# The second MLP matrix of a decoder block: the seven products of a unit in another order

## The chip, the cores and the metric

The kernel runs on one core of one Trainium2 chip. The metric is the device time of one launch in microseconds (us), lower is better; it is taken over several runs, and the median is given with the lowest and the highest. A profile shows one further execution of the same program with every instruction's start and length on the core's engines: TensorE (PE; its weight loads are listed apart, as PEld), VectorE (DVE), ScalarE (ACT), GpSimd (POOL) and SyncE (SP). SP and POOL serve here mainly as queues from which transfers are issued.

## What is computed

One layer of a decoder block for 512 tokens of width 2048, in float32: a mixing part (gated convolution beside attention), then a dense MLP with a squared ReLU, then a last normalisation. The change lies in the MLP:

```python
h = rmsnorm(x, g_mlp[l])
u = jnp.square(jax.nn.relu(jnp.einsum('bsd,df->bsf', h, w_ff1[l])))
x = x + jnp.einsum('bsf,fd->bsd', u, w_ff2[l])
return rmsnorm(x, g_final)
```

`w_ff1` is 2048 x 8192 and `w_ff2` 8192 x 2048. The second product, `u` times `w_ff2`, is "the second MLP matrix".

## The kernel before

**Seven products in place of eight.** Matrix products are cut into 2 x 2 blocks, and a block product is made with seven multiplications of sums of blocks (the Strassen-Winograd scheme). The kernel names the multiplications after the operand on the side of `u`: A11, A12, A22 are blocks of `u` themselves, S1 to S4 are sums of blocks. On the side of the weights, A11 is multiplied with the block X00, A12 with X10, S4 with X11, S1 with X01 - X00, S3 with X11 - X01, S2 with X11 - (X01 - X00), called t2, and A22 with X10 - t2.

**Float32 from two parts.** Each weight operand is split before it is multiplied (`split`, line 99, called by `run`, line 970): ScalarE copies it, rounded, into `th`, and VectorE writes the remainder into `tl`. There are two buffers of each. `mm_rows` (line 145) then issues 24 matmuls of 128x512 a product, for each of two halves of the tokens eight with `th` (lines 156 and 157) and four with `tl` (line 159).

**Sums on the side of `u`.** While the first MLP matrix runs, `put_u` (line 829) squares the results, makes the sums S1 to S4 and stores all seven operands side by side in one DRAM tile per segment (`s_d`, seven places of 256 columns). `load_sums` (line 896) brings them back through POOL's queue in four transfers of neighbouring places, into the four tiles that the table `US` (line 894) names: two operands, two, two, and one. Each tile is free again when its last product of the segment before is done.

**Units.** The second matrix runs over eight segments of 1024 rows of `w_ff2` and, in each, over two groups of 1024 columns: 16 units (`unit`, line 954). A unit

- loads its four blocks of `w_ff2` through SP's queue (line 967), in the order of the loop in line 962, into four rotating buffers; a buffer goes back to the list `free` after the last use of its block, and the next unit's loads take the buffers in the order in which they were given back;
- runs the seven products (lines 989 to 1018) into three PSUM tiles: `a` takes A11, S2, S1 and S4 one on top of the other, `d` takes S3 and A22, `b` takes A12 and is kept through all segments;
- between products overwrites blocks with their differences (`sub`, line 103: X00 becomes X01 - X00, X01 becomes X11 - X01, and t2 is a tile of its own), and adds the PSUM tiles into the output rows held in SBUF (`into`, line 978; line 107 is the addition). In the first segment the first write of each output quarter is a copy on ScalarE.

In the last segment the evictions do more: `residual` (line 940) loads the residual stream in a piece (`old`, on POOL's queue) and adds it to the rows, and `finish` (line 929) scales and adds the last product, has ScalarE sum the squares, and multiplies with the final gain. After the last unit the rows are normalised and written out, rows 2 and 3 of four first.

**What sets the order.** The code gives the instructions of all engines in one sequence. When the program is built, each engine's queue is put in an order by the code's sequence and by when operands are expected to be ready, so a queue may hold a later instruction of the code ahead of an earlier one. On the chip each engine works its queue in that order, with waits on the others.

Of the kernel before, what the change touches and what calls it, by code (L numbers as in the profile page):

```python
# [11 lines left out]
AF = mybir.ActivationFunctionType  # L12
# [33 lines left out]
def tile_hybrid_block(ctx: ExitStack, tc, x, g_mix, w_in, b_f, b_gate, conv_w, w_conv_out,  # L46
                      w_attn_out, w_mix_out, g_mlp, w_ff1, w_ff2, g_final, out):
    nc = tc.nc
    x, out = x[0], out[0]
# [49 lines left out]
    def split(src, hi, lo):  # L99
        nc.scalar.activation(out=hi, in_=src, func=AF.Copy)  # L100
        nc.vector.tensor_tensor(out=lo, in0=src, in1=hi.bitcast(F32), op=ALU.subtract)  # L101

    def sub(out, a, b):
        nc.vector.tensor_tensor(out=out, in0=a, in1=b, op=ALU.subtract)  # L104

    def add(out, a, b):
        nc.vector.tensor_tensor(out=out, in0=a, in1=b, op=ALU.add)  # L107

    def parts(shape, at=0):

        q, w = shape[1:]
        return tuple(main.tile([P, WBUF], F32R, tag=tag, name=tag, bufs=2)[:, at:at + q * w]
                     .rearrange("p (q c) -> p q c", q=q) for tag in ("th", "tl"))
# [31 lines left out]
    def mm_rows(ps, Sx, hi, lo, first):  # L145

        nq, w = hi.shape[1], hi.shape[2]
        for b in range(2):
            o = ps[b][:, :w] if len(ps) == 2 else ps[0][:, b * w:(b + 1) * w]
            begin = first and (b == 0 or len(ps) == 2)  # L150
            ts = slice(b * P, (b + 1) * P)
            for part in range(2):
                for q in range(nq):
                    Sh, Sl = (e[:, ts] for e in Sx(q))
                    if part == 0:
                        nc.tensor.matmul(o, Sh, hi[:, q, :], start=begin and q == 0, stop=False, skip_group_check=True)  # L156
                        nc.tensor.matmul(o, Sl, hi[:, q, :], start=False, stop=False, skip_group_check=True)  # L157
                    else:
                        nc.tensor.matmul(o, Sh, lo[:, q, :], start=False, stop=q == nq - 1, skip_group_check=True)  # L159
# [6 lines left out]
    free, later = [0, 1, 2, 3], []  # L166
# [159 lines left out]
    def rstd_of(part):  # L326
        v = stat.tile([P, 1], F32, tag="v", name="v")
        nc.vector.tensor_reduce(out=v, in_=part, axis=AX.X, op=ALU.add)
        r = stat.tile([P, 1], F32, tag="r", name="r")
        nc.gpsimd.tensor_tensor(out=r, in0=v, in1=mhalf, op=ALU.pow)  # L330
        return r
# [307 lines left out]
    for c in range(4):  # L639
        held = main.tile([P, 4, S], F32, tag="x1", name="held")  # L640
# [186 lines left out]
    held = []  # L827

    def put_u(g):
        quarters = {}  # L830

        def square(v, out):
            nc.scalar.activation(out=out, in_=v, func=AF.Square)

        def sums(j):
            r = pf.tile([P, 7, HS], F32, tag="r", name="r")
            if j == 0:
                nc.scalar.activation(out=r[:, 0:6:5], in_=held.pop(0), func=AF.Copy)
            else:
                square(quarters[0, j], r[:, 0:6:5])  # L840
            low = quarters[1, j]
            square(low[:, 1, :], r[:, 3, :])
            square(low[:, 0, :], low[:, 0, :])
            add(r[:, 4, :], low[:, 0, :], r[:, 3, :])
            sub(r[:, 1, :], r[:, 0, :], low[:, 0, :])
            sub(r[:, 2, :], r[:, 4, :], r[:, 0, :])
            sub(r[:, 6, :], r[:, 5, :], r[:, 2, :])
            h = pf.tile([P, 7, HS], F32R, tag="rh", name="rh")
            nc.scalar.activation(out=h, in_=r, func=AF.Copy)
            nc.vector.tensor_tensor(out=r, in0=r, in1=h.bitcast(F32), op=ALU.subtract)  # L850
            q = 2 * (g % 2) + j
            nc.gpsimd.dma_start(out=s_d[g // 2][:, 0, q], in_=h.bitcast(F32))
            nc.gpsimd.dma_start(out=s_d[g // 2][:, 1, q], in_=r)

        def hold():
            c = pf.tile([P, 2, HS], F32, tag="c", name="c")
            square(quarters[0, 0], c)
            held.append(c)

        def put(i, j, v):  # L860
            nc.scalar.activation(out=v, in_=v, func=AF.Relu, scale=common)  # L861
            quarters[i, j] = v
            if (i, j) == (0, 0):
                later.append(hold)
            elif j == 0:
                later.append(lambda: sums(0))
            elif (0, 1) in quarters and (1, 1) in quarters:
                sums(1)

        return put  # L870
# [20 lines left out]
    for g in heads:  # L891
        g.tail()

    US = ((4, ("A11", "S3")), (5, ("S2", "A22")), (6, ("S1", "A12")), (2, ("S4",)))

    def load_sums(seg, ks, ST):

        for k in ks:
            place, names = US[k]
            t = main.tile([P, 2, 4, len(names), HS], F32R, tag=f"t{place}", name="us")  # L900
# [28 lines left out]
    def finish(i, j, cg, ps):  # L929

        c = 2 * cg + j
        for e in range(2):
            t = 2 * i + e
            xs = x1[t][:, c * S:(c + 1) * S]
            nc.vector.scalar_tensor_tensor(out=xs, in0=ps[:, e], scalar=turned[:, t:t + 1], in1=xs, op0=ALU.mult, op1=ALU.add)  # L935
            square_part(xs, ss3[:, t, c:c + 1], otile([P, S], "junk"))
            if (i, c) != (0, 3):
                nc.vector.tensor_tensor(out=xs, in0=xs, in1=gf[:, c * S:(c + 1) * S], op=ALU.mult)

    def residual(i, j, cg):  # L940

        c = 2 * cg + j
        old = pg.tile([P, 2, S], F32, tag="old", name="old", bufs=2)
        nc.gpsimd.dma_start(out=old, in_=x1_d[2 * i:2 * i + 2, :, c * S:(c + 1) * S].rearrange("t p c -> p t c"))
        for e in range(2):
            t = 2 * i + e
            xs = x1[t][:, c * S:(c + 1) * S]
            nc.vector.scalar_tensor_tensor(out=xs, in0=xs, scalar=turned[:, t:t + 1], in1=old[:, e], op0=ALU.mult,
                                           op1=ALU.add)

    def banks2(i, name):
        return pairs.tile([P, 2, S], F32, tag=f"q{i}", name=name)

    def unit(seg, cg, ST):


        a, d = banks2(cg, "a"), banks2(1 - cg, "d")
        if seg == 0:
            kept[cg] = banks2(2 + cg, "b")
        b = kept[cg]  # L960
        X, at = {}, {}
        for i, j in ((0, 0), (0, 1), (1, 1), (1, 0)):
            at[i, j] = free.pop(0)
            t = main.tile([P, 4, S], F32, tag=f"x{at[i, j]}", name=f"y{i}{j}")
            c = NW * cg + S * j
            src = w_ff2[seg * 1024:(seg + 1) * 1024, c:c + S].rearrange("(q two p) c -> two p q c", two=2, p=P)
            nc.sync.dma_start(out=t, in_=src[i])
            X[i, j] = t

        def run(ps, n, src, first):  # L970
            hi, lo = parts([P, 4, S])
            split(src, hi, lo)
            mm_rows((ps[:, 0], ps[:, 1]), ST[n], hi, lo, first)

        last = seg == NSEG - 1
        begun = set()

        def into(i, j, ps, end=False):
            c = NW * cg + S * j
            xs = xp[i][:, :, c:c + S]  # L980
            if last and end:
                finish(i, j, cg, ps)
            elif seg == 0 and (i, j) not in begun:
                nc.scalar.activation(out=xs, in_=ps, func=AF.Copy)
            else:
                add(xs, ps, xs)
            begun.add((i, j))

        run(a, "A11", X[0, 0], True)
        sub(X[0, 0], X[0, 1], X[0, 0])  # L990
        sub(X[0, 1], X[1, 1], X[0, 1])
        into(0, 0, a)
        run(d, "S3", X[0, 1], True)
        free.append(at[0, 1])
        t2 = main.tile([P, 4, S], F32, tag="t3", name="t2")
        sub(t2, X[1, 1], X[0, 0])
        into(1, 1, d)
        run(a, "S2", t2, False)
        sub(t2, X[1, 0], t2)
        into(1, 0, a)  # L1000
        if last:
            residual(1, 0, cg)
        run(d, "A22", t2, False)
        into(1, 0, d, True)
        if last:
            residual(1, 1, cg)
        run(a, "S1", X[0, 0], False)
        free.append(at[0, 0])
        into(1, 1, a, True)
        if last:  # L1010
            residual(0, 0, cg)
        run(b, "A12", X[1, 0], seg == 0)
        free.append(at[1, 0])
        if last:
            into(0, 0, b, True)
            residual(0, 1, cg)
        run(a, "S4", X[1, 1], False)
        free.append(at[1, 1])
        into(0, 1, a, True)
# [13 lines left out]
    for t in (2, 3, 0, 1):  # L1033
        r = rstd_of(ss3[:, t, :])
# [43 lines left out]
```

## Time and profile before

| | us |
|---|---|
| median of three runs | 2507.99 |
| lowest, highest | 2504.74, 2508.36 |
| the profiled execution | 2509.61 |
| its span, first to last instruction | 2507.9 |
| granted TensorE clock, mean | 0.996 of full speed |

In the profile, L12 means line 12 of the kernel as printed above; `out<-in` gives the tiles by the program's names, where `us` are the operands on the side of `u`, `y` the blocks of `w_ff2`, `t` the tile t2, `x` (with `a`, `b`, `d`) the output rows, and `th`, `tl` the split parts. In a timeline a row is: start in us from the span's start, length, engine, line, operation, tiles, shape, how many instructions the row stands for, and in brackets how long the engine was idle before and what ended that. In a table of windows a row is: the window, its length, then for each engine its busy time with the count of instructions, the granted TensorE clock, the mean busy share of the DMA engines and the GB/s that they moved. A matmul's length is modelled and overlaps the next one's; the distance between starts is what it costs.

### The profile page before, as it was taken

The numbers are of one execution on the slowest core, as the hardware profiler recorded it, in microseconds if no ns is written. First come the engines' busy times: TensorE is split into PE (matmuls) and PEld (weight loads), VectorE is DVE, ScalarE is ACT, GpSimd is POOL, SyncE is SP. The second block draws the span as 40 slices with busy tenths as digits, with TensorE's granted clock in tenths as the row PEclk, the third lists the DMA queues.
The fourth block names the chain that finished last, engine by engine and source line by source line (L and its number), as shares of the span: only waits on it lengthen the run. The fifth ranks groups of instructions, "written<-read, shape, count | busy, mean of one in ns | idle before, by whom it ended". The sixth has DMA issues, their size and how long they took to land. (4 is left out here: it accounts for less than half of the span.)

```text
span 2507.9 us, 39017 instructions
## 1 busy us (share of the span) xinstructions
PE 2453.0 (98%) x16911; PEld 2255.6 (90%) x16911; DVE 1902.2 (76%) x1498; ACT 1149.7 (46%) x1136; POOL 112.4 (4%) x184
## 2 busy tenths in 40 slices
PE   8999999999999999999999999999999999999997
PEld 7999989999999988888889999999998878787785
DVE  7877677789767744435678888898887877878888
ACT  6443434334444622235556666666664333333343
POOL 0000000000000000000000000000011000000010
PEclk9999999999999999999999999999999999999999
DMA  7554444456543554435654655646688557665573
GB/s 242 163 174 156 155 133 147 139 180 207 165 137 120 190 173 137 146 133 201 202 170 181 223 182 197 242 172 217 219 307 282 162 190 238 214 213 158 187 257 107
DMA packets 289919, 465.06 MB, mean 185 GB/s; under 512 B 10236, under 2 KB 194644, under 8 KB 289620
## 3 DMA queue, kind: packets, MB, share of 16 engines
q1 hardware_dynamic: 260704, 330.40, 41.2%
q0 software_dynamic: 28176, 131.08, 14.0%
q8 instruction: 132, 2.16, 0.4%
q10 hardware_dynamic: 868, 1.10, 0.1%
q14 instruction: 39, 0.32, 0.0%
HBM read 370.26 MB, written 92.27 MB: 184 GB/s over the span
## 5 line engine op out<-in xcount | busy, mean ns | idle before, releaser
L101 DVE TENSOR_TENSOR tl<-x,th 128x2048 fp32r<-128x2048 f32 (+1 forms) x252 | 574.7, 2288 | 216.6 <-ACT th L100 198.7
L100 ACT ACTIVATE th<-x 128x2048 fp32r<-128x2048 f32 (+1 forms) x252 | 482.4, 1917 | 498.5 <-PE a L141 184.8
L104 DVE TENSOR_TENSOR x<-x,x 128x2048 f32<-128x2048 f32 (+1 forms) x144 | 329.2, 2286 | 14.8 <-DMA x<-in_w_in_dram 7.1
L100 ACT ACTIVATE th<-y 128x2048 fp32r<-128x2048 f32 x80 | 153.7, 1921 | 271.3 <-DVE y L104 102.6
L101 DVE TENSOR_TENSOR tl<-y,th 128x2048 fp32r<-128x2048 f32 x80 | 182.8, 2284 | 47.3 <-ACT th L100 47.3
L101 DVE TENSOR_TENSOR tl<-raw,th 128x2048 fp32r<-128x2048 f32 x40 | 91.7, 2292 | 152.0 <-ACT th L100 151.5
L156 PE MATMUL a<-th,us 128*128 128x512 f32 x512 | 200.9, 392 | 3.0 <-ACT o L861 1.5
L157 PE MATMUL a<-th,us 128*128 128x512 f32 x512 | 199.4, 389 | 0.0
L139 PE MATMUL a<-ST,th 128*128 128x256 f32 x768 | 181.6, 281 | 5.9 <-ACT th L100 5.9
L141 PE MATMUL a<-ST,th 128*128 128x256 f32 x768 | 181.1, 280 | 0.0
L100 ACT ACTIVATE th<-raw 128x2048 fp32r<-128x2048 f32 x40 | 76.7, 1918 | 175.5 <-PE pt L302 62.6
L139 PEld LDWEIGHTS a<-ST,th 128*128 128x128 f32 x768 | 146.5, 191 | 6.6 <-ACT th L100 6.5
L141 PEld LDWEIGHTS a<-ST,th 128*128 128x128 f32 x768 | 146.5, 191 | 0.0
L139 PE MATMUL a<-S,th 128*128 128x256 f32 x576 | 134.1, 278 | 5.5 <-ACT th L100 5.5
L159 PE MATMUL a<-tl,us 128*128 128x512 f32 x512 | 136.9, 389 | 0.1
L141 PE MATMUL a<-S,th 128*128 128x256 f32 x576 | 133.5, 277 | 0.0
L156 PEld LDWEIGHTS a<-th,us 128*128 128x128 f32 x512 | 96.1, 188 | 28.5 <-ACT th L100 6.1
L139 PE MATMUL d<-ST,th 128*128 128x256 f32 x512 | 119.1, 278 | 0.0
L141 PE MATMUL d<-ST,th 128*128 128x256 f32 x512 | 119.1, 278 | 0.0
L159 PEld LDWEIGHTS a<-tl,us 128*128 128x128 f32 x512 | 96.0, 188 | 20.7 <-DVE tl L101 0.9
L139 PEld LDWEIGHTS a<-S,th 128*128 128x128 f32 x576 | 108.2, 188 | 6.8 <-ACT th L100 6.5
L157 PEld LDWEIGHTS a<-th,us 128*128 128x128 f32 x512 | 96.1, 188 | 19.6
(284 smaller groups left out, 6237.6 us busy)
## 6 DMA issues: line engine op xcount, KB each, us to landing
x<-in_w_in_dram SPq DMA_DIRECT2D x86, 1024.0 KB, 5.9
x<-in_w_ff_dram SPq DMA_DIRECT2D x66, 1024.0 KB, 7.8
y<-in_w_ff_dram SPq DMA_DIRECT2D x64, 1024.0 KB, 6.2
us<-s_d POOLq DMA_DIRECT2D x48, 1024.0 KB, 8.9
s_d<-rh POOLq DMA_DIRECT2D x32, 896.0 KB, 5.0
s_d<-r POOLq DMA_DIRECT2D x32, 896.0 KB, 8.2
raw<-in_w_mix_out_dram SPq DMA_DIRECT2D x24, 1024.0 KB, 5.1
g_d<-o SPq DMA_DIRECT2D x32, 256.0 KB, 2.2
```

The source lines that it names most:

```text
L100: nc.scalar.activation(out=hi, in_=src, func=AF.Copy)
L101: nc.vector.tensor_tensor(out=lo, in0=src, in1=hi.bitcast(F32), op=ALU.subtract)
L104: nc.vector.tensor_tensor(out=out, in0=a, in1=b, op=ALU.subtract)
L139: nc.tensor.matmul(o, hi[:, q, js], Sh, start=first and q == 0 and j == 0, stop=False, skip_group_check=True)
L141: nc.tensor.matmul(o, hi[:, q, js], Sl, start=False, stop=False, skip_group_check=True)
L156: nc.tensor.matmul(o, Sh, hi[:, q, :], start=begin and q == 0, stop=False, skip_group_check=True)
L157: nc.tensor.matmul(o, Sl, hi[:, q, :], start=False, stop=False, skip_group_check=True)
L159: nc.tensor.matmul(o, Sh, lo[:, q, :], start=False, stop=q == nq - 1, skip_group_check=True)
```

## The change

The products of a unit run in the order A11, A12, S2, S3, S1, A22, S4 instead of A11, S3, S2, A22, S1, A12, S4. With it move:

- the places of the stored operands, in `put_u` and in `US`, so that each of the four transfers of a segment again holds the operands in the order of use;
- the loads of the four blocks: X00, X10, X01, X11 instead of X00, X01, X11, X10;
- the subtraction X11 - X01, now behind S2, and the point at which X10's buffer is given back, now behind X10 - t2;
- the evictions, each still behind its product, and in the last segment the `residual` and `finish` steps.

```diff
@@ put_u, sums(j)
-                nc.scalar.activation(out=r[:, 0:6:5], in_=held.pop(0), func=AF.Copy)
+                nc.scalar.activation(out=r[:, 0:2], in_=held.pop(0), func=AF.Copy)
             else:
-                square(quarters[0, j], r[:, 0:6:5])
+                square(quarters[0, j], r[:, 0:2])
             low = quarters[1, j]
-            square(low[:, 1, :], r[:, 3, :])
+            square(low[:, 1, :], r[:, 5, :])
             square(low[:, 0, :], low[:, 0, :])
-            add(r[:, 4, :], low[:, 0, :], r[:, 3, :])
-            sub(r[:, 1, :], r[:, 0, :], low[:, 0, :])
+            add(r[:, 4, :], low[:, 0, :], r[:, 5, :])
+            sub(r[:, 3, :], r[:, 0, :], low[:, 0, :])
             sub(r[:, 2, :], r[:, 4, :], r[:, 0, :])
-            sub(r[:, 6, :], r[:, 5, :], r[:, 2, :])
+            sub(r[:, 6, :], r[:, 1, :], r[:, 2, :])
@@
-    US = ((4, ("A11", "S3")), (5, ("S2", "A22")), (6, ("S1", "A12")), (2, ("S4",)))
+    US = ((4, ("A11", "A12")), (5, ("S2", "S3")), (6, ("S1", "A22")), (2, ("S4",)))
@@ unit
-        for i, j in ((0, 0), (0, 1), (1, 1), (1, 0)):
+        for i, j in ((0, 0), (1, 0), (0, 1), (1, 1)):
@@
         run(a, "A11", X[0, 0], True)
         sub(X[0, 0], X[0, 1], X[0, 0])
-        sub(X[0, 1], X[1, 1], X[0, 1])
         into(0, 0, a)
-        run(d, "S3", X[0, 1], True)
-        free.append(at[0, 1])
+        if last:
+            residual(0, 0, cg)
+        run(b, "A12", X[1, 0], seg == 0)
+        if last:
+            into(0, 0, b, True)
         t2 = main.tile([P, 4, S], F32, tag="t3", name="t2")
         sub(t2, X[1, 1], X[0, 0])
-        into(1, 1, d)
         run(a, "S2", t2, False)
+        sub(X[0, 1], X[1, 1], X[0, 1])
         sub(t2, X[1, 0], t2)
+        free.append(at[1, 0])
         into(1, 0, a)
         if last:
             residual(1, 0, cg)
-        run(d, "A22", t2, False)
-        into(1, 0, d, True)
+        run(d, "S3", X[0, 1], True)
+        free.append(at[0, 1])
+        into(1, 1, d)
         if last:
             residual(1, 1, cg)
         run(a, "S1", X[0, 0], False)
         free.append(at[0, 0])
         into(1, 1, a, True)
         if last:
-            residual(0, 0, cg)
-        run(b, "A12", X[1, 0], seg == 0)
-        free.append(at[1, 0])
-        if last:
-            into(0, 0, b, True)
             residual(0, 1, cg)
+        run(d, "A22", t2, False)
+        into(1, 0, d, True)
         run(a, "S4", X[1, 1], False)
         free.append(at[1, 1])
         into(0, 1, a, True)
```

## Prediction

> **What bounds the kernel now.** First the page's head and busy shares, then windows over the stage of the second MLP matrix, then the timelines of TensorE, VectorE and ScalarE inside it.
>
> ```profile
> span 2507.9 us, 39017 instructions
> PE 2453.0 (98%) x16911; PEld 2255.6 (90%) x16911; DVE 1902.2 (76%) x1498; ACT 1149.7 (46%) x1136; POOL 112.4 (4%) x184
> ```
> TensorE (PE) is the bound of the whole. The windows cut the stage into its first three units, then eleven like units, and the two units of the last segment:
>
> ```profile
> core 0: us, PE busy (x) PEld busy (x) DVE busy (x) ACT busy (x) POOL busy (x), PEclk, DMA share, GB/s
> 1864.40:1983.50 119.10, 118.48 (x519) 97.21 (x520) 93.81 (x53) 53.43 (x36) 11.40 (x17) 1.00 0.74 254
> 1983.50:2409.80 426.30, 422.65 (x1836) 342.76 (x1836) 344.15 (x187) 147.88 (x77) 34.27 (x46) 1.00 0.62 206
> 2409.80:2494.90 85.10, 79.41 (x335) 63.10 (x333) 81.85 (x77) 35.78 (x44) 7.40 (x10) 0.98 0.36 118
> ```
> In the eleven units VectorE (DVE) works 344.15 of 426.3 us (81%), so there it only delays PE where the order is unlucky; in the last segment it works 81.85 of 85.1, so there it is the bound. Where PE stands still is in its timeline. The rows are first matmuls: A11 of the first four units, A11 of the last unit of segment 6, its S3, an early piece of S2, the second half of S2, and the next unit's A11.
>
> ```profile
> 1864.42 0.47 PE L156 MATMUL a<-th,us 128*128 128x512 f32 x1 [1.47 <-ACT o L861]
> 1903.85 0.39 PE L156 MATMUL a<-th,us 128*128 128x512 f32 x1
> 1941.99 0.39 PE L156 MATMUL a<-th,us 128*128 128x512 f32 x1
> 1980.15 0.39 PE L156 MATMUL a<-th,us 128*128 128x512 f32 x1
> ...
> 2370.36 0.39 PE L156 MATMUL a<-th,us 128*128 128x512 f32 x1
> 2376.22 0.50 PE L156 MATMUL d<-th,us 128*128 128x512 f32 x1 [0.25 <-ACT th L100]
> 2378.41 0.50 PE L156 MATMUL a<-th,us 128*128 128x512 f32 x1
> 2384.90 0.39 PE L156 MATMUL a<-th,us 128*128 128x512 f32 x1
> 2409.38 0.39 PE L156 MATMUL a<-th,us 128*128 128x512 f32 x1
> ```
> From 2384.90 to 2409.38 PE does half of S2 and four whole products, 108 matmuls of the unit's 168, in 24.48 us: 0.2267 us each, 5.44 a product (24). A unit without a stall would take 38.08, and two did: 1903.85 to 1941.99 is 38.14, to 1980.15 is 38.16. This one took 2409.38 - 2370.36 = 39.02. S3 was due at 2370.36 + 5.44 = 2375.80 and began at 2376.22. So **0.87 us a unit** (39.02 - 38.15) is lost between A11 and S3, where the row names ScalarE's `th` as what came last. Why it is late (ScalarE row, then VectorE's, then ScalarE's again):
>
> ```profile
> 2364.22 1.92 ACT L100 ACTIVATE th<-y 128x2048 fp32r<-128x2048 f32 x1 [3.52 <-PE b L157]
> ...
> 2366.17 2.29 DVE L101 TENSOR_TENSOR tl<-y,th 128x2048 fp32r<-128x2048 f32 x1 [3.06 <-ACT th L100]
> 2368.50 2.29 DVE L104 TENSOR_TENSOR y<-y,y 128x2048 f32<-128x2048 f32 x1
> 2370.71 1.22 DVE L107 TENSOR_TENSOR x<-a,x 128x1024 f32<-128x1024 f32 x1
> 2371.84 2.28 DVE L104 TENSOR_TENSOR y<-y,y 128x2048 f32<-128x2048 f32 x1
> 2374.04 2.29 DVE L104 TENSOR_TENSOR t<-y,y 128x2048 f32<-128x2048 f32 x1
> 2376.24 1.22 DVE L107 TENSOR_TENSOR x<-a,x 128x1024 f32<-128x1024 f32 x1
> 2377.38 2.28 DVE L101 TENSOR_TENSOR tl<-y,th 128x2048 fp32r<-128x2048 f32 x1
> ...
> 2374.24 1.93 ACT L100 ACTIVATE th<-y 128x2048 fp32r<-128x2048 f32 x1 [8.10 <-DVE y L104]
> ```
> It is one chain: A11's split may start only at 2364.22, when product A12's two `th` halves are read and one of the two `th` buffers is free; then its `tl`, the overwrite of X00 (2368.50), the last eviction of the unit before (2370.71), X01's overwrite (2371.84), and only then S3's `th`, which ends 2376.17. It has two products to hide behind (S4 and A11) and is 0.42 too long; S3's `tl` (2377.38 to 2379.66) is then late too, and that is the rest. The rows show also that VectorE's queue isn't in the order of the code: the subtraction for S2 (2374.04) stands ahead of A11's eviction (2376.24), which the code has first. An instruction goes ahead when its inputs are there earlier.
>
> **The change, part by part.** The counts stay: seven splits, four subtractions and six evictions of 128x1024 a unit in segments 0 to 6, the same matmuls, loads and bytes. Only order and due times move, so each price is a stall gained or lost.
>
> *Second product A12 in place of S3.* A12 is a loaded block, not a difference: its `th` needs one landed load and a `th` buffer, free when the previous unit's S4 is 4.53 us in, 0.9 before A11. No chain is left there. Gain 0.87 a unit if nothing else takes its place.
>
> *Third product S2.* Its chain is A11's `tl`, X00's overwrite, X11 - X00, `th`. I lay the eleven units out by the rows' durations (2.2 us from one wide VectorE instruction to the next, 1.13 an eviction), offsets from PE's start of A11 as in the rows: A11's `tl` -4.2, X00 -1.9 to 0.35, eviction to 1.5, A12's `tl` to 3.7, X11 - X00 to 5.9, S2's `th` 6.0 to 7.9. S2 is due at 10.88: 2.9 us spare, against 0.42 missing before. Then A11's eviction to 7.1, X01's overwrite to 9.3, S2's `tl` to 11.5 (due 10.88 + 1.81 = 12.69), S3's `th` 10.2 to 12.1, X10 - t2 to 13.8, S3's `tl` to 16.0 (S3 due at 16.32). From there each product has only eviction and `tl` ahead of it, as S1, A12 and S4 have in the trace, none of which stalls. So the stall goes, and nothing is late in its stead: 11 x 0.87 = **9.6 us**. From above the gain is bounded by 11 x (39.02 - 38.08) = 10.3.
>
> *Loads and stored sums.* X10 moves from fourth to second, X11 from third to fourth. The fourth load takes the buffer that S4's `tl` leaves, near 31.8 after A11 (2399.84 + 2.28 - 2370.36, below; S4 is seventh in both orders), and is now due for X11 - X00 at 3.7 of the next unit, at 41.9; before, the fourth load was X10, first due for X10 - t2, after S2's `tl`, more than three products into the next unit's work. It is 10.1 us to that, and 12.9 until PE would notice (the 2.9 spare). S4's `tl`, and landing times in the source view of the tile, then of the load at that place in a segment's last unit, and of one without company:
>
> ```profile
> 2399.84 2.28 DVE L101 TENSOR_TENSOR tl<-y,th 128x2048 fp32r<-128x2048 f32 x1
> ...
> DMA to landing us min/median/max: 2.0/6.2/16.4
> ...
> y<-in_w_ff_dram SPq DMA_DIRECT2D x1, 1024.0 KB, 11.1
> ...
> y<-in_w_ff_dram SPq DMA_DIRECT2D x1, 1024.0 KB, 6.2
> ```
> The 6.2 is hidden. The 11.1 is 1.0 later than VectorE would like and inside PE's spare; cost 0. If a load took the 16.4, it would be 3.5 a time, at the seven segment borders. The stored sums change places only inside one 128x1792 tile, and each product finds its sums in the transfer of the same rank as before: products one and two in the first, three and four in the second. The queues of SP and POOL keep their lengths: 0, covered by those four-product leads; uncovered, one transfer's landing.
>
> *Units of segment 0.* The first takes 39.43 (1864.42 to 1903.85), the next two have nothing to lose. Between 0 and 1.3 to gain; the first has other work of the stage before on VectorE, so I take 0.
>
> *The last segment.* Its evictions become `finish` and `residual`, and these move: A11's and A12's ahead of S2, A22's to just before S4.
>
> ```profile
> 2424.37 1.42 DVE L948 SCALAR_TENSOR_TENSOR x<-x,turned,old 128x512 f32<-128x512 f32 x2
> ...
> 2452.41 1.40 DVE L935 SCALAR_TENSOR_TENSOR x<-a,turned,x 128x512 f32<-128x512 f32 x2
> 2453.73 2.28 DVE L104 TENSOR_TENSOR y<-y,y 128x2048 f32<-128x2048 f32 x1
> 2455.93 1.28 DVE L938 TENSOR_TENSOR x<-x,gf 128x512 f32<-128x512 f32 x2
> ...
> 2458.06 0.79 PE L156 MATMUL d<-th,us 128*128 128x512 f32 x1 [3.70 <-ACT th L100]
> ...
> 2461.57 0.63 PE L159 MATMUL d<-tl,us 128*128 128x512 f32 x2
> ...
> 2455.00:2465.00 10.00, 6.94 (x23) 5.61 (x24) 7.93 (x7) 3.83 (x2) 0.00 (x0) 0.83 0.01 2
> ```
> A residual is 1.42 us and a finish 1.40 + 1.28 in the same queue as the splits; the longest wait (3.70) is S3's `th` behind them. With VectorE full (81.85 of 85.1) and its work the same, the segment's length stays: 0. It could be 8.9 shorter (2 x 38.08 = 76.2 is PE alone) or longer, as in the second rival; nearest is the full engine, so I keep 0, and 4 us either way for the forecast's own range.
>
> *The end.* Rows 2 and 3 of the output now get their last piece after A22, not S1.
>
> ```profile
> 2490.75 1.40 DVE L935 SCALAR_TENSOR_TENSOR x<-b,turned,x 128x512 f32<-128x512 f32 x2
> 2492.07 0.21 DVE L328 TENSOR_REDUCE v<-ss 128x1 f32<-128x5 f32 x2
> ...
> 2492.24 0.64 ACT L334 ACTIVATE junk<-x 128x512 f32<-128x512 f32 x1
> ```
> Their sum of squares (2492.07) will wait for what stands now at 2490.75 and for its square, to 2492.9: 0.9 later. It lies beside S4's end, at 2494.9; between 0 and 0.9, I take 0.5.
>
> **Sum**: 9.6 + 0 + 0 + 0 - 0.5 = 9.1 us less. Against the profiled execution's 2509.61 (span 2507.9 and 1.7 around it) that is 2500.5; its time lies 1.6 above the median of the three runs (2507.99), against which it is 2498.9. I take **2499.5**.
>
> **The rivals.**
> *1. The stall moves to S2: no change.* If VectorE's queue holds X11 - X00 behind A11's eviction (ready at 5.6) and X01's overwrite, it ends at 11.2, and `th` at 13.2, 2.3 late; behind the eviction alone and with half a microsecond of hand-offs it is about 0.7 late, near the 0.87 of now. Time then 2507. For it: the new chain uses the same engine in the same microseconds. Against: the row of 2374.04 stood ahead of the eviction.
>
> *2. The last segment pays: slower.* The place is A12's finish ahead of S2's subtraction, in the two last units. If the queue is in the code's order there, PE waits after A12 for 1.40 + 2.28 + 1.92 and 0.2 of hand-offs, 5.8 us, twice. After the wait of 3.70 the clock in its window was 0.83 and eight matmuls took 3.5 us (2458.06 to 2461.57) in place of 1.8, so some 1.6 more each: 14.8 in all, less 9.1 gained: 2507.99 + 5.7, about 2513.5. It decides once finish(0,0) is queued before the subtraction. For it: the code has that order, and a full VectorE leaves no slack. Against: the subtraction's inputs are there 5 us earlier, and such pairs changed places above.
> The Trainium skill, "TensorE: Matmul & The Clock Gate", section "HAM oscillation — how this bites in real kernels", warns of TensorE gaps over about 3.4 us, after which its clock falls. The trace agrees: 1.00 in the windows with the short stalls, 0.83 after the 3.70; by that rule both waits would be charged, as the price above does.
>
> *3. X11 lands late at segment borders: slower.* At seven borders 3.5 us each if the 16.4 came every time: 24.5 - 9.1, so 2523; at 14 us of landing it is 1.1 each, 7.7, and the time is 2506.5. For it: the 11.1. Against: the four loads of a unit now have all but one landed before it, since X01's and X10's are issued ahead of the second transfer of sums.
> The Trainium skill, "DMA: Bandwidth & Descriptors", section "Queues, rings and completion order", says that an engine takes turns packet by packet between the queues that have work, so such a load keeps no precedence over the sums. The 11.1 beside 6.2 agrees.
>
> **How the numbers follow.** Forecast 0.62, with an own range of 2495 to 2504; rival 1 0.14; rival 2 0.14; rival 3 0.10. A measurement of this kernel tells about 0.2% (5 us) from no change. Faster by more: the forecast but for 0.01 at its edge, 0.61. Within: that 0.01, most of rival 1 (0.11) and half of rival 3 (0.05), 0.17. Slower: rival 2, the other half of rival 3 and 0.03 of rival 1 (the 2.3 late), 0.22. The range goes from 2495 (all stalls gone and a shorter last segment) to 2512, which leaves out most of rival 2 and the worst of rival 3.
>
> **What will show it.** Right: A11 to A11 of 38.15 in the units from segment 1 on, no wait of PE between A11 and S3, `th` of S2 some 3 us ahead of its matmul, a last segment near 85. Wrong: a wait at S2 of 0.7 or more in each unit (rival 1); gaps over 3 us after A12 in the last two (rival 2); VectorE waiting for a load at X11 - X00 (rival 3).

## The result and the profile after

| | before | after |
|---|---|---|
| median of six runs, us | 2508.18 | 2497.84 |
| lowest, highest | 2504.41, 2511.37 | 2493.34, 2499.86 |
| the profiled execution | 2509.61 | 2499.57 |
| its span | 2507.9 | 2497.8 |

The ratio is 0.9958, with an interval from 0.9944 to 0.9972: between 7.0 and 14.0 us less. The head and the busy shares of the page after, then the windows of the same three parts of the stage (the columns are those of before):

```profile
span 2497.8 us, 39035 instructions
PE 2444.2 (98%) x16911; PEld 2255.4 (90%) x16911; DVE 1902.0 (76%) x1498; ACT 1149.4 (46%) x1136; POOL 112.5 (5%) x184
```
```profile
1860.80:1976.80 116.00, 115.94 (x505) 95.87 (x506) 90.46 (x51) 51.96 (x36) 10.60 (x16) 0.99 0.73 257
1976.80:2395.70 418.90, 418.90 (x1850) 346.87 (x1849) 347.08 (x188) 147.97 (x78) 34.35 (x46) 1.00 0.60 210
2395.70:2484.70 89.00, 79.87 (x337) 63.33 (x335) 82.15 (x76) 34.83 (x43) 7.00 (x10) 0.98 0.34 112
```
The counts and VectorE's busy time are as before. In the eleven units PE is now busy for all of the 418.90 us; before, it was 422.65 of 426.3. The last two units are longer, 89.0 against 85.1. The unit starts in PE's timeline, with S2's first matmul in the last unit of segment 6:

```profile
1860.87 0.77 PE L156 MATMUL a<-th,us 128*128 128x512 f32 x1 [2.36 <-ACT o L861]
...
1976.79 0.39 PE L156 MATMUL a<-th,us 128*128 128x512 f32 x1
...
2357.59 0.39 PE L156 MATMUL a<-th,us 128*128 128x512 f32 x1
...
2368.47 0.39 PE L156 MATMUL a<-th,us 128*128 128x512 f32 x1
...
2395.67 0.39 PE L156 MATMUL a<-th,us 128*128 128x512 f32 x1
```
From 2357.59 to 2395.67 is 38.08, exactly 168 matmuls of 0.2267, and so is each of the thirteen units from the second on. S2 begins 10.88 after A11, two products later to the hundredth: nothing waits in between. With the rows of before this gives the account of the difference of the two profiled spans:

| part of the span | before | after | difference |
|---|---|---|---|
| up to the stage's first matmul | 1864.42 | 1860.87 | -3.55 |
| units 1 to 3 | 115.73 | 115.92 | +0.19 |
| eleven units | 429.23 | 418.88 | -10.35 |
| the two units of the last segment | 85.48 | 88.97 | +3.49 |
| after the last matmul | 13.05 | 13.17 | +0.12 |
| sum | 2507.9 | 2497.8 | -10.1 |

Two entries were not in the sum of the prediction: the last segment's, and the first, which lies ahead of the stage that was changed. The last segment is in three timelines. VectorE's (the rows 2425.25 and 2427.90 are those of L948, `residual`, and L935, `finish`), then POOL's transfers of `old` with the landing times from the view of that tile, then PE's:

```profile
2416.55 1.41 DVE L948 SCALAR_TENSOR_TENSOR x<-x,turned,old 128x512 f32<-128x512 f32 x2
...
2420.64 1.22 DVE L107 TENSOR_TENSOR x<-d,x 128x1024 f32<-128x1024 f32 x1 [0.49 <-PE d L159]
2425.25 2.74 DVE L948 SCALAR_TENSOR_TENSOR x<-x,turned,old 128x512 f32<-128x512 f32 x4 [3.38 <-DMA old<-x_d]
2427.90 1.40 DVE L935 SCALAR_TENSOR_TENSOR x<-a,turned,x 128x512 f32<-128x512 f32 x2
2429.22 2.28 DVE L101 TENSOR_TENSOR tl<-t,th 128x2048 fp32r<-128x2048 f32 x1
```
```profile
2418.25 0.72 POOL L944 DMA_DIRECT2D old<-x_d  x1 [10.88 <-DVE x L948]
...
DMA to landing us min/median/max: 4.0/5.0/7.0
```
```profile
2425.66 0.39 PE L157 MATMUL d<-th,us 128*128 128x512 f32 x1
2429.41 0.47 PE L156 MATMUL a<-th,us 128*128 128x512 f32 x1 [3.36 <-ACT junk L334]
2431.77 1.91 PE L159 MATMUL d<-tl,us 128*128 128x512 f32 x4
```
Read it from the load. There are two buffers `old`. The fourth residual of unit (7,0), residual(0,1), uses the one that residual(1,0) frees at the end of the row 2416.55, so its transfer is issued at 2418.25, and the longest of the four landings is 7.0 us: 2425.25, the moment at which VectorE goes on. In VectorE's queue the first half of residual(0,1) stands ahead of residual(1,1), of its own second half (the row's four pieces), of finish(1,1) and of A22's `tl`. So A22's eight first matmuls end at 2425.9; S4's first ones, which PE's queue has next, start only when finish(1,1) has emptied tile `a` (2427.90 + 1.40 = 2429.30), and A22's part with `tl` starts at 2431.77. PE stands for 3.5 us. Its row names ScalarE's square, `junk`, which came from the same finish. Before, a wait of that size also stood in this segment (3.70, at S3), with only one more, of 1.6, behind it; here three more of 2.2, 1.8 and 1.5 follow in the last unit.

### The profile page after: what moved, and what is told of

Read it like the earlier page. It is cut to its first block, busy times and chain, and to the rows that moved or that the text cites. A ratio compares the mean times of both kernels' runs of the same rounds, so it can differ in the third digit from the quotient of the medians.

```text
span 2497.8 us, 39035 instructions
## 1 busy us (share of the span) xinstructions
PE 2444.2 (98%) x16911; PEld 2255.4 (90%) x16911; DVE 1902.0 (76%) x1498; ACT 1149.4 (46%) x1136; POOL 112.5 (5%) x184
## 3 DMA queue, kind: packets, MB, share of 16 engines
q1 hardware_dynamic: 260704, 330.40, 40.8%
## 4 chain that ended last, share of the span: by engine, by line
PE 72%; DVE 4%; DMA 3%; issue 2%; ACT 1%; POOL 0%; SPq 0%; POOLq 0%; ACTq 0%; DVEq 0%
PE a L139 5%; PE a L141 5%; PE a L143 5%; PE a L156 4%; PE a L157 4%; PE a L159 4%; PE d L141 3%; PE d L139 3%; PE d L143 3%; PE pt L301 2%; PE pn L310 2%; PE pn L308 2%; PE pt L303 2%; PE pn L309 2%; PE pt L302 2%; PE d L159 2%
## 5 line engine op out<-in xcount | busy, mean ns | idle before, releaser
L139 PE MATMUL a<-ST,th 128*128 128x256 f32 x768 | 178.7, 278 | 5.8 <-ACT th L100 5.8
L141 PE MATMUL a<-ST,th 128*128 128x256 f32 x768 | 178.3, 278 | 0.0
L100 ACT ACTIVATE th<-t 128x2048 fp32r<-128x2048 f32 x32 | 61.4, 1919 | 135.2 <-DVE t L104 68.9
```

Source lines behind the costliest of these rows:

```text
L139: nc.tensor.matmul(o, hi[:, q, js], Sh, start=first and q == 0 and j == 0, stop=False, skip_group_check=True)
L141: nc.tensor.matmul(o, hi[:, q, js], Sl, start=False, stop=False, skip_group_check=True)
```

## The experiments

The first four runs are about the two unforeseen entries, the other six about the chain and the order. A unit's length is the distance from A11 to A11 in PE's timeline, as above. Where one time is given without a range or a ratio, the kernel ran once. Beside S2 second, A12 second, the longer chain of S2 and the loads in the order of before stood one run of the kernel before, of 2510.48; beside the work off the chain and the shortened chain of S3, eleven with a median of 2504.26.

**Both kernels once more**, unchanged, in a second comparison with 20 runs of the kernel before (median 2505.11), which the next two kernels share.

> The kernel before, unchanged, profiled once more. In the profile of the changed kernel the stretch of the first MLP matrix (1250 to 1500 us) is 4 to 7 us shorter than in the profile of before, though the instructions there are the same: matmuls of 128x256 took 276 ns on average there and 281 ns before. Theory one: that belongs to the single execution, and this run shows some 276 ns and 444 matmuls in 50 us from 1350 on, with the second matrix as before (39.02 from A11 to A11, a last segment near 85). Theory two: it belongs to the kernel, and 281 ns and 427 matmuls come again.

> The changed kernel, unchanged, beside the next two on the same chip. Theory: 9 to 10 us under before, by units of 38.08 in place of 39.02 (11 of them, 10.3) less 3.5 lost in the last segment, plus what the first matrix's rate gives by chance. If the 4 us of the first matrix are chance, the ratio should come nearer to 0.9975 (6 us) than to 0.996 (10 us).

The kernel after has 2497.25 in nine runs, ratio 0.9965 [0.9942, 0.9988]. The second pair of profiles has spans of 2502.1 and 2495.5, 6.6 apart: -10.27 in the eleven units (429.15 against 418.88), +2.96 in the last segment (85.51 against 88.47), -0.54 in the first three units, +1.0 behind the last matmul, and +0.25 ahead of the stage, where the first pair had -3.55. That piece is placed by windows over 150 us of the first MLP matrix, of before, after and before again:

```profile
1350.00:1500.00 150.00, 150.00 (x1278) 150.00 (x1277) 127.97 (x94) 91.38 (x93) 7.98 (x15) 1.00 0.56 197
```
```profile
1350.00:1500.00 150.00, 150.00 (x1325) 150.00 (x1324) 132.11 (x100) 94.84 (x95) 8.01 (x15) 1.00 0.58 207
```
```profile
1350.00:1500.00 150.00, 149.66 (x1319) 149.47 (x1319) 131.47 (x100) 94.85 (x95) 7.99 (x15) 1.00 0.58 206
```
In the first execution of before PE was busy all the time and still did only 1278 matmuls; the other two did 1325 and 1319. That stretch has the same instructions in both kernels; only the places differ into which `put_u` writes the operands. Over the eight profiles with the new places the stage starts anywhere between 1855.49 and 1865.03 (mean 1860.1), over the three with the old ones between 1859.63 and 1864.42 (mean 1862.5). A spread of up to 9.5 us in one layout is more than the 3.55, so this piece need not be an effect of the change; that the places have none, of a us or two, isn't shown. What the change does from there on is 6.6 us in the first pair (-10.35 + 3.49 + 0.19 + 0.12) and 6.9 in the second (-10.27 + 2.96 - 0.54 + 1.0).

**The last segment in the order of before**, all other segments in the new one.

```diff
-        for i, j in ((0, 0), (1, 0), (0, 1), (1, 1)):
+        for i, j in (((0, 0), (0, 1), (1, 1), (1, 0)) if seg == NSEG - 1 else ((0, 0), (1, 0), (0, 1), (1, 1))):
...
+        if last:
...
+            return
```
(In the branch stand the products, subtractions and evictions of before, in their order.)

> The new order in segments 0 to 6, the old order of products, loads, residual and finish steps in the last segment. Theory: gain and loss are separate; the units from segment 1 on stay at 38.08 and the last segment returns from 89.0 to some 85.5, so 3 to 4 us under the changed kernel. Rival: the last segment is set by VectorE's sum alone, the same in both orders, and the 3.5 came from the state in which the segment starts; then it stays near 89 and the time is that of the changed kernel.

The eleven units stay at 418.88, and the last two take 85.59, as before the change. The wait at S3 is back with its row, 3.69 against 3.70:

```profile
2437.52 0.79 PE L156 MATMUL d<-th,us 128*128 128x512 f32 x1 [3.69 <-ACT th L100]
```
So the order of the last two units is what cost 3 us. The time, 2497.02 with ratio 0.9969 [0.9957, 0.9981], cannot be told from that of the kernel after: an effect this small is in the traces, not in the medians.

**Residual(0,1) of unit (7,0) in two spare buffers** of the output, meant to let its load wait for no other residual.

```diff
+        if (i, j, cg) == (0, 1, 0):
+            halves = [otile([P, S], "old") for e in range(2)]
+            for e in range(2):
+                nc.gpsimd.dma_start(out=halves[e], in_=x1_d[2 * i + e, :, c * S:(c + 1) * S])
+        else:
...
```

> The changed kernel, but the residual piece of the first last-segment unit's quarter (0,1) is loaded as two halves into spare output buffers and no longer into the pair of buffers that the three other pieces share. Theory: the last segment's loss is one wait, VectorE's 3.38 us for that load ahead of A22's split; without it TensorE's 3.5 us wait in A22 goes and the last segment is 85 to 86 us, 3 to 3.5 us under the changed kernel. Rival: VectorE is full there and the wait only comes elsewhere; last segment 88 to 89, no change.

```profile
2415.62 2.28 DVE L101 TENSOR_TENSOR tl<-t,th 128x2048 fp32r<-128x2048 f32 x1
2417.82 1.41 DVE L954 SCALAR_TENSOR_TENSOR x<-x,turned,old 128x512 f32<-128x512 f32 x2
2419.15 1.40 DVE L935 SCALAR_TENSOR_TENSOR x<-a,turned,x 128x512 f32<-128x512 f32 x2
...
2426.19 1.41 DVE L954 SCALAR_TENSOR_TENSOR x<-x,turned,old 128x512 f32<-128x512 f32 x2 [2.25 <-DMA old<-x_d]
```
A22's `tl` (2415.62) goes ahead of residual(1,1) and residual(0,1) now, finish(1,1) follows, and VectorE waits for the load (2426.19) when the two splits that PE needs next are done. The load itself is later than it was. POOL's queue has it behind one for the next unit, which waits for a residual:

```profile
2419.53 0.70 POOL L949 DMA_DIRECT2D old<-x_d  x1 [6.76 <-DVE x L954]
2420.22 1.12 POOL L946 DMA_DIRECT2D old<-x_d  x2
```
It landed at 2426.19, 36.7 us after the first matmul of the last segment (2389.47); in the kernel after it was 29.6 (2425.25 against 2395.67). So the edit brought the load later, not sooner; it moved the residual behind A22's `tl` in VectorE's queue, and there the late load holds up less. An earlier load with the queue as it was has not been run. The last two units take 85.91: of the 3.5 us, 3.1 are gone. In the last unit one wait of 3.7 for A12's `tl` (2440.44) now stands where there were two, of 2.2 and 1.8. The new order with this one load moved has 2492.76 (2489.34 to 2499.44), ratio 0.9955 [0.9938, 0.9971]: the lowest median of all, 12.4 us under before beside it. Against the kernel after the intervals overlap. Giving `old` a third buffer was not tried.

**S2 second, A12 third**: the chain's product in the place that A12 has taken.

```diff
-        run(b, "A12", X[1, 0], seg == 0)
...
         sub(t2, X[1, 1], X[0, 0])
         run(a, "S2", t2, False)
+        run(b, "A12", X[1, 0], seg == 0)
```

> Products in the order A11, S2, A12, S3, S1, A22, S4, all else as in the changed kernel. Theory: the stall of before comes from a product that stands second and whose operand is a difference; S2's chain (A11's tl, X00's overwrite, one eviction, X11 - X00, th) is as long as S3's was, so S2 begins some 0.4 us late and the units from segment 1 on take 38.9 to 39.1 again. Rival: the gain came from the new places of the loads or of the evictions, which stay; then 38.08.

It took 2542.97, more than expected: from segment 1 on PE stood 1.9 us ahead of the second product in each second unit of a segment, and from 1.8 to 5.8 in the first ones. VectorE's timeline, then PE's, then VectorE's at a border:

```profile
2156.80 2.28 DVE L104 TENSOR_TENSOR t<-y,y 128x2048 f32<-128x2048 f32 x1
2159.00 2.28 DVE L104 TENSOR_TENSOR y<-y,y 128x2048 f32<-128x2048 f32 x1
2161.20 1.22 DVE L107 TENSOR_TENSOR x<-a,x 128x1024 f32<-128x1024 f32 x1
```
```profile
2162.57 0.47 PE L156 MATMUL a<-th,us 128*128 128x512 f32 x1 [1.73 <-DVE x L107]
```
```profile
2198.23 2.29 DVE L104 TENSOR_TENSOR t<-y,y 128x2048 f32<-128x2048 f32 x1 [1.26 <-DMA y<-in_w_ff_dram]
```
What ends last is no longer `th`: S2 is added up in the same PSUM tile `a` as A11, so it must wait for A11's eviction (2161.20), and that stands in VectorE's queue behind both subtractions. The unit takes 40.1, the 1.9 and 0.1 of slower first matmuls over 38.08. With A12 between them, as in the change, the eviction lies beside A12's 5.44 us. At this border X11 was late for the subtraction as well, the mechanism of the third rival, in an order that needs X11 one product earlier.

**A12 second and the rest as before** (A11, A12, S3, S2, A22, S1, S4), with loads and stored sums in that order.

```diff
-    US = ((4, ("A11", "S3")), (5, ("S2", "A22")), (6, ("S1", "A12")), (2, ("S4",)))
+    US = ((4, ("A11", "A12")), (5, ("S3", "S2")), (6, ("A22", "S1")), (2, ("S4",)))
...
         into(0, 0, a)
...
+        run(b, "A12", X[1, 0], seg == 0)
...
+        sub(X[0, 1], X[1, 1], X[0, 1])
         run(d, "S3", X[0, 1], True)
```

> Products in the order A11, A12, S3, S2, A22, S1, S4, loads and stored sums to match: the order of before with only A12 moved up. Theory: A12 in second place is all that is needed, S3 third has over 2.9 us to spare, and the units take 38.08 as in the changed kernel. Rival: S2 in third place or S3 in fourth matters too; then between 38.1 and 39.0.

2517.11, with units of 39.49. The stall at S3 is gone, but a new one of 1.4 stands at the other end of the unit:

```profile
2169.91 1.07 PE L159 MATMUL a<-tl,us 128*128 128x512 f32 x4
2172.08 0.50 PE L156 MATMUL a<-th,us 128*128 128x512 f32 x1 [1.10 <-ACT th L100]
```
```profile
2170.11 1.91 ACT L100 ACTIVATE th<-y 128x2048 fp32r<-128x2048 f32 x1 [3.52 <-PE a L157]
```
```profile
2171.02 1.23 DVE L107 TENSOR_TENSOR x<-a,x 128x1024 f32<-128x1024 f32 x1 [2.02 <-PE a L159]
```
S1 ends at 2170.82 (four matmuls from 2169.91). S4 follows it in tile `a`, and S1's eviction runs from 2171.02 to 2172.25. The row of 2172.08 names ScalarE's `th`, because PE's queue holds two matmuls of the next unit's A11 there, ahead of S4 (ten matmuls with `th` run before the next four with `tl`, where a half product has eight); but the eviction alone would hold S4 to 2172.25. The 1.41 by which the unit exceeds 38.08 is the hand-off and the eviction, 0.2 + 1.23. So moving A12 alone trades the one stall for another; the order of the change also keeps S1 and S4 apart, with A22 between.

**S2's chain longer by one subtraction**: X11 - X00 is made twice, with the same result.

```diff
-        sub(t2, X[1, 1], X[0, 0])
+        for _ in range(2):
+            sub(t2, X[1, 1], X[0, 0])
```

> The changed kernel with X11 - X00 made twice, into the same tile. Theory: S2's split has 2.9 us to spare before TensorE is held up. The second subtraction stands behind A11's eviction, so S2's th ends 3.3 us later, at 11.3 after A11 where it is due at 10.88, and its tl 2.2 later, at 13.7 where it is due at 12.7: units of 38.5 to 39.1. Rival: the spare is over 3.3 us, or VectorE's order gives way; then 38.08.

```profile
2219.48 2.28 DVE L104 TENSOR_TENSOR t<-y,y 128x2048 f32<-128x2048 f32 x1
2221.68 1.22 DVE L107 TENSOR_TENSOR x<-a,x 128x1024 f32<-128x1024 f32 x1
2222.82 2.28 DVE L104 TENSOR_TENSOR t<-y,y 128x2048 f32<-128x2048 f32 x1
```
```profile
2225.21 1.92 ACT L100 ACTIVATE th<-t 128x2048 fp32r<-128x2048 f32 x1 [8.27 <-DVE t L104]
```
```profile
2227.19 0.50 PE L156 MATMUL a<-th,us 128*128 128x512 f32 x1 [0.42 <-ACT th L100]
```
A11's eviction came between the two, so the chain grew by 2222.82 - 2219.48 = 3.34. S2 began 0.59 late: the spare was 3.34 - 0.59 = 2.75, against 2.9 predicted. Units became 39.18 to 39.21, and the time 2516.55. It is the length of this chain that decides, not the amount of work, as the next run shows from the other side.

**The same amount of work off the chain**: one more wide subtraction, over X00 after S1's split, where it is read no more.

```diff
         run(a, "S1", X[0, 0], False)
+        sub(X[0, 0], X[1, 1], X[1, 1])
         free.append(at[0, 0])
```

> The changed kernel with one more wide subtraction a unit, as in chain_plus1, but over X00 after S1's split, where no product waits for it. Theory: what counts is the chain, not the amount of VectorE's work (33.6 of 38.1 us); units of 38.08. Rival: VectorE's amount counts as such; 38.5 to 39.2 as in chain_plus1.

```profile
1980.00:2396.00 416.00, 416.00 (x1837) 344.77 (x1836) 368.38 (x197) 146.82 (x77) 34.26 (x46) 1.00 0.62 211
```
VectorE works 368 us of 416 there, 89%, and PE none the less without a gap: every unit is 38.08. In the last segment, where VectorE was full, the two extra subtractions of 2.2 cost 6.4 (95.36 against 88.97). The time was 2507.63.

**The loads in the order of before**, the products in the new one.

```diff
-        for i, j in ((0, 0), (1, 0), (0, 1), (1, 1)):
+        for i, j in ((0, 0), (0, 1), (1, 1), (1, 0)):
```

> The changed order of products with the loads in the order of before (X00, X01, X11, X10), so that X10 comes fourth and is due for the second product. Theory: inside a segment the 6.2 us of landing are hidden and the unit takes 38.08; at the seven segment borders the load takes 8 to 11 us beside the sums' transfers, A12's th begins up to 1.3 us late, and the first unit of a segment takes 38.1 to 39.7. Rival: the landing is too late in every unit (38.5 and more throughout), or in none (38.08 throughout).

38.08 in all units from the second to the fourteenth, at borders too, and 2499.95. From the second unit to the end of segment 6 the order of the loads neither costs nor gives anything; a cost at the borders was expected and is not there. The last segment was 89.64, 0.7 and 1.2 over the two executions of the kernel after, in one execution.

**The order of before, with S3's chain shortened**: X11 - X01 is made into t2 at once, and no longer waits for X00's overwrite.

```diff
+        t2 = main.tile([P, 4, S], F32, tag="t3", name="t2")
+        sub(t2, X[1, 1], X[0, 1])
         sub(X[0, 0], X[0, 1], X[0, 0])
-        sub(X[0, 1], X[1, 1], X[0, 1])
-        into(0, 0, a)
-        run(d, "S3", X[0, 1], True)
         free.append(at[0, 1])
-        t2 = main.tile([P, 4, S], F32, tag="t3", name="t2")
+        into(0, 0, a)
+        run(d, "S3", t2, True)
         sub(t2, X[1, 1], X[0, 0])
```

> The order of products, loads and sums of before; only S3's operand X11 - X01 is made into the tile t2 instead of over X01, so that it no longer waits for A11's tl and for the overwrite of X00. Theory: the 0.87 to 0.94 us of each unit came from that chain alone; S3's th then waits only for its buffer, and the units from segment 1 on take 38.1 as in the changed kernel, with the last segment of before (85.5): 2495 to 2498, 10 us under before. At segment borders X11 may land late and cost up to 2 us. Rival: the old order has another stall behind this one (S3's tl, or t2's second use for S2); units between 38.3 and 39.0.

Half of it came true. From segment 1 on second units of a segment are 38.08: with a shorter chain the old order has no stall either. But first units are 40.8 to 42.6, and the time is 2527.93, ratio 1.0091 [1.0065, 1.0116]. VectorE at a border, then PE:

```profile
2186.65 2.29 DVE L104 TENSOR_TENSOR t<-y,y 128x2048 f32<-128x2048 f32 x1 [6.19 <-DMA y<-in_w_ff_dram]
2188.86 2.28 DVE L101 TENSOR_TENSOR tl<-y,th 128x2048 fp32r<-128x2048 f32 x1
```
```profile
2191.20 1.20 PE L159 MATMUL a<-tl,us 128*128 128x512 f32 x4 [1.51 <-DVE tl L101]
```
The subtraction is queued ahead of A11's own `tl` now, and its blocks haven't landed when a segment begins: VectorE stands 6.19 us, and A11 waits for its `tl`. At the border to segment 1 it is the same (5.79). At the four others up to segment 6 VectorE stands 4.4 to 4.9 us; A11 gets its `tl` in time or nearly so, and the delay shows behind it, as waits of 0.4 and 0.2 us in the rows of S2 and of A22. An order that asks for no difference until the third product, as the change has it, doesn't meet this.

## Why the prediction came out as it did

**The stall between A11 and S3.** Right, in cause and place. Shown by three runs: the stall goes when S3's chain is shortened (second units of 38.08), it comes back at S2 when that chain is made longer than its spare, and it doesn't come from more VectorE work off the chain. The gain was taken as 0.87 a unit, to 38.15, and came out as 0.94, to the 38.08 of pure matmul time: 10.35 us for eleven units, at the upper bound of 10.3 instead of 9.6.

**Nothing late in its stead.** Right. The layout by hand can be laid beside the timelines of VectorE and ScalarE (A11 at 2357.59):

```profile
2361.35 2.29 DVE L104 TENSOR_TENSOR t<-y,y 128x2048 f32<-128x2048 f32 x1
2363.55 1.22 DVE L107 TENSOR_TENSOR x<-a,x 128x1024 f32<-128x1024 f32 x1
2364.68 2.28 DVE L104 TENSOR_TENSOR y<-y,y 128x2048 f32<-128x2048 f32 x1
2366.88 2.28 DVE L101 TENSOR_TENSOR tl<-t,th 128x2048 fp32r<-128x2048 f32 x1
```
```profile
2363.75 1.93 ACT L100 ACTIVATE th<-t 128x2048 fp32r<-128x2048 f32 x1 [4.95 <-DVE t L104]
```
X11 - X00 ends 6.05 after A11 (5.9 predicted), S2's `th` runs from 6.16 to 8.09 (6.0 to 7.9), S2's `tl` ends at 11.57 (11.5). The spare is 10.88 - 8.09 = 2.8. The subtraction stands ahead of A11's eviction and of X01's overwrite, which was the case against the first rival.

**Loads and stored sums at 0.** Right for the units of segments 0 to 6: the first unit after a border is 38.08 like the others, with the loads in either order. The third rival's late X11 is a real mechanism of this kernel, seen where X11 is due earlier (S2 second, S3 early), but not in the change. In the profile after, X11 as the fourth load landed in 6.2 to 7.5 us at the seven borders and not in the 11.1 that the prediction took from the kernel before; the slowest loads of the stage, up to 13.9, were X01's, the third. The 16.4 of the rival's upper price belongs to a load issued ahead of the stage; within the stage the longest of before was 11.1.

**Units of segment 0 at 0.** About right: +0.19 and -0.54 for the three in the two pairs of profiles. The +0.19 holds some 1.6 us of slow first matmuls (last section).

**The last segment at 0.** This step failed: "With VectorE full (81.85 of 85.1) and its work the same, the segment's length stays". The work did stay the same (82.15), the length grew by 3.5 and 3.0, inside the 4 that was allowed either way. A full engine bounds a stretch from below only; a wait in its queue comes on top. The wait is for a load that the prediction followed nowhere: in the new order residual(0,1) stands in VectorE's queue ahead of the split that A22 needs, and its load can only start when residual(1,0) has freed the buffer. The second rival had the segment and the direction, but not the mechanism: finish(0,0) was not queued ahead of S2's subtraction in either unit.

**The end at +0.5.** +0.1 and +1.0 behind the last matmul, on both sides of the value and near the bounds of 0 and 0.9; whether the later sum of squares made it wasn't followed.

**The sum.** Predicted were 9.1 us less; the stage and the end gave 6.6 and 6.9. The two profiled executions lie 10.1 apart only because the one of before was 3.55 later ahead of the stage. The medians lie 10.3 apart in the first comparison and 7.9 in the second; the 6.6 and 6.9 lie inside the second's interval (3.0 to 14.5) and just under the first's (7.0 to 14.0). So it is in part luck that the predicted 2499.5 came within 2 us of 2497.84: the 3 us lost in the last segment, which the sum put at nothing, were made up by a difference that the changed stage doesn't show.

## What to carry to other kernels

Where products of different preparation share an engine, find the one whose operand passes through the longest chain of instructions, put a product that needs no preparation behind the start, and count for each next product when its chain ends and when it is due: laid out by hand from measured durations, that was right here to 0.2 us. Count the accumulator among the operands: two products that follow each other in one PSUM tile have the first one's eviction between them, so a product for another tile belongs there. And for a stretch in which an engine is full, look at every load that its queue waits for, at which instruction frees that load's buffer and at what stands behind the wait in the queue, before calling the length unchanged.

## What the hardware showed besides

The windows of the first MLP matrix above give a granted clock of 1.00 in all three executions, yet one of them did 3.5% fewer matmuls in 150 us without a gap. What slowed it can't be seen in these traces.

A short wait of PE can cost more than its length. The stage's first matmul in the kernel after came after a wait of 2.36 us (1860.87, above). In its second profiled execution the same row of PE's timeline is:

```profile
1859.88 0.47 PE L156 MATMUL a<-th,us 128*128 128x512 f32 x1 [1.50 <-ACT th L100]
```
After the 2.36 the first eight matmuls took 3.45 us instead of 1.81, in a window (1858 to 1866) with a granted clock of 0.79, and the first unit 39.76; after the 1.50 it took 38.18. The run with work off the chain had 2.80 there, a first row of 0.77 too and a first unit of 39.77; ten of the twelve profiles had 1.62 or less, and 0.47.

The length of the wait alone doesn't decide it. In the second execution of before the wait of 3.70 ahead of S3 in the last unit came again, and the clock around it stayed at 1.00:

```profile
2452.34 0.50 PE L156 MATMUL d<-th,us 128*128 128x512 f32 x1 [3.70 <-ACT th L100]
...
2448.00:2458.00 10.00, 5.87 (x25) 4.18 (x24) 9.03 (x7) 3.67 (x6) 0.00 (x0) 1.00 0.01 2
```
The eight matmuls behind it took 1.95 us, where those of the first execution took 3.5 at 0.83. With S2 second, a wait of 2.55 (2366.71) left the clock at 1.00 too. What else decides isn't shown. Nor did the slow matmuls lengthen the last segment of before, where VectorE is the bound: it took 85.48 with them and 85.51 without, so the 1.6 that the second rival charged behind each wait is no sure cost.

The Trainium skill, "TensorE: Matmul & The Clock Gate", section "HAM oscillation — how this bites in real kernels", puts the limit at gaps of about 3.4 us. The wait in the last segment of the kernel after, 3.36 in its row, lies at that limit, and the clock fell (0.84 from 2425 to 2436). The 2.36 and the 2.80 were enough below it, and one of the two waits of 3.70 was not enough above it; for these the measurement decides.
